# Where four stationary operands lie in SBUF: a two-layer decoder trunk with the start addresses of xh, xl, yh and yl moved by 16 to 64 bytes

## The chip, the cores and the metric

The kernel runs on one core of a Trainium2 chip. The metric is the device time in microseconds of one execution. Before the change the median of three runs is 935.96 us (935.75 to 936.89).

## The reference

The reference computes a causal decoder trunk of two layers over 256 positions of width 2,048, in float32. Cut to what matters:

```python
def layer_even(x, norm_g, w_in, w_out):          # layer 0
    h = rmsnorm(x, norm_g)
    qa, ka, va, iq, ik, iw, qb, kb, vb, gate = split_cols(h @ w_in, SPLIT0)
    ...                                          # mixer A: top-64 sparse attention, 10 heads
    ...                                          # mixer B: dilated windows, 6 heads
    y = jnp.concatenate([o_a, o_b], axis=-1)
    return x + (y * jax.nn.silu(gate)) @ w_out

def layer_odd(x, norm_g, w_in, b_f, w_out):      # layer 1
    ...                                          # the same with stick-breaking and forgetting attention
    return x + (y * jax.nn.silu(gate)) @ w_out

def reference(x, ...):
    x = layer_even(x, norm0, w_in0, w_out0)
    x = layer_odd(x, norm1, w_in1, b_f1, w_out1)
    return rmsnorm(x, norm_f)
```

Nearly all arithmetic is in the four products `h @ w_in` and `y @ w_out`: 256 rows by 2,048 by some 20,000 columns of weights in all.

## The kernel before

**Jobs.** The columns of the four weight matrices are sorted into 39 jobs of mostly 512 columns: 14 for layer 0's input projection (one for each head or pair of heads, K with 336 columns for the shared keys, I0 and I1 for the indexer), P0 to P3 for its output projection, 17 for layer 1's input projection (F1 with 264 columns and G1 with 256 among them), and Q0 to Q3 for its output projection. `project` (L303) runs a job: 16 k tiles of 128, for each of them two tiles of 128 positions (`th`).

**The product.** A float32 product is made of three single-pass products in the type fp32r. A weight tile is split into a high and a low part, `whi` and `wlo`, by ScalarE (L265) and VectorE (L266), two k tiles at a time; the input has been split in the same way into `xh` and `xl` (inputs of both input projections) or `yh` and `yl` (inputs of both output projections). `product` (L298 to L301) then issues

```python
nc.tensor.matmul(o, a, wh, ...)   # L299: a = xh or yh
nc.tensor.matmul(o, a, wl, ...)   # L300: a = xh or yh
nc.tensor.matmul(o, b, wh, ...)   # L301: b = xl or yl
```

The second argument, 128 x 128 of the input, is the stationary operand: it is loaded into the array ahead of each matmul (LDWEIGHTS rows, PEld in the profile). The third, a row of split weights (a "row" is one k tile of a job: 512 columns, 2,048 bytes in a partition), is streamed through. There is such a load for each matmul, since two neighbours never share one instruction. The loads of x and y tiles take 128 x 4 = 512 bytes out of each partition, those of neighbouring `th` and k lying 512 bytes apart.

**Where it lies.** The Tile pools hand out SBUF in the order of the code. Before, `align_bytes=PHASE` with PHASE = 512 puts the four inputs at multiples of 512 bytes in a partition, and a tile `fill` of 88 floats (L209) brings the weights' buffers `raw`, `whi` and `wlo` behind them to multiples of 512 as well. The rows in `whi` and `wlo` follow one another without a gap, so every row of 512 or 256 columns starts at a multiple of 512; every second row of F1 (264 columns, 1,056 bytes) starts 32 over one, every second row of K (336 columns, 1,344 bytes) 320 over. The indexer's `ih` and `il` (loaded at L530 to L532) lie 192 over. In bytes from the start of a partition, with the rest against 512:

| tile | before | rest | after | rest |
|---|---|---|---|---|
| xh | 16,896 | 0 | 16,864 | 480 |
| xl | 33,792 | 0 | 33,312 | 32 |
| yh | 50,688 | 0 | 50,112 | 448 |
| yl | 67,584 | 0 | 66,576 | 16 |
| cons, xs | 83,968, 96,256 | 0 | 82,976, 95,264 | 32 |
| raw, first whi, first wlo | 115,200, 139,776, 156,160 | 0 | 114,688, 139,264, 155,648 | 0 |

**Order of the work.** The order is written by hand (`manual_schedule`). While `project` walks through a job, `tick` advances the attention work of earlier jobs, which is written as generators and yields its instructions between the job's matmuls: transposes (L357, L603), scores, weighted sums. Splits run three halves ahead (AHEAD, L295). The room of yh and yl serves in the first job as landing place for eight k tiles of weights each (`home`, tiles w0yh and w0yl), and yh and yl are allocated over it once that job is done (L773). In the last job, Q3, the room of xh and xl takes split weights of the first eight k tiles (L256 to L258), and the second tile of positions is done in two halves of 256 columns.

Of the kernel before, what the change touches and what calls it, by code (L numbers as in the profile page):

```python
# [7 lines left out]
F32 = mybir.dt.float32  # L8
BF16 = mybir.dt.bfloat16
F32R = mybir.dt.float32r  # L10
# [4 lines left out]
P = 128  # L15
NT = 2
SEQ = 256
D = 2048
KT = D // P
# [133 lines left out]
    t = np.concatenate([t, ci, si], 1)  # L153
    return np.ascontiguousarray(t.reshape(NT, P, -1).transpose(1, 0, 2).reshape(P, -1))

PHASE = 512


@with_exitstack
def trunk(ctx, tc, x, xT, g1, w0, wo0, w1, wo1, bf, gf, consts, rope, out):  # L160
    nc = tc.nc
    cp = ctx.enter_context(tc.tile_pool(name="cp", bufs=1))
# [4 lines left out]
    pa = ctx.enter_context(tc.tile_pool(name="pa", bufs=2, space=PSUM))  # L167
    ctx.enter_context(tc.manual_schedule())

    xh, xl = (cp.tile([P, KT, SEQ], F32R, name=n, align_bytes=PHASE) for n in ("xh", "xl"))  # L170
    home = [cp.tile([P, KT * SEQ], F32, name=f"w0{n}", tag=n, align_bytes=PHASE) for n in ("yh", "yl")]
    ys = []
    cons = cp.tile([P, CW], F32, name="cons")
    rt = cp.tile([P, NT, RW // 2], F32, name="rt")
# [31 lines left out]
    logf = cp.tile([P, NT, HDD], F32, name="logf")  # L206
    cq = cp.tile([P, NT, HDD], F32, name="cq")
    cT = score[0:HDD, 0:SEQ]
    cp.tile([P, 88], F32, name="fill")  # L209
    cTd = dr.tile([HDD, SEQ], F32, name="cTd")  # L210
    r0, r1, r2 = rstd[:, 0, :], rstd[:, 1, :], rstd[:, 2, :]
    BLK = ((0, slice(0, P)), (1, slice(P, 384)))
# [62 lines left out]
    def start(g):  # L275
        n = next(g, None)
        if n is not None:
            side.append([g, n])
# [24 lines left out]
    def project(ji):  # L303
        _, (w, _), name, which = jobs[ji]
        ah, al = ys if which else (xh, xl)
        ps = [pj.tile([P, 512], F32, name=f"pj{th}", tag=f"pj{th}") for th in range(NT)]
        mine = [i for i in range(hidx[0], len(halves)) if halves[i][0] == ji]
        hidx[0] = mine[-1] + 1

        def kts(i, ths, cs=slice(0, w)):  # L310
            _, _, kt0, _, m = halves[i]
            hi, lo = parts[i]
            for j in range(m):
                kt = kt0 + j
                for th in ths:
                    t = slice(th * P, (th + 1) * P)
                    product(ps[th][:, cs], ah[:, kt, t], al[:, kt, t], hi[:, j * w:(j + 1) * w][:, cs],
                            lo[:, j * w:(j + 1) * w][:, cs], kt)
                tick(w * len(ths) / 2)

        if name == "Q3":
            for i in mine:
                split(i + 1 + AHEAD)
                kts(i, (0,))
            finish(ps, 0)
            for c2 in range(2):
                if c2:
                    ps[1] = pj.tile([P, 512], F32, name="pj1", tag="pj1")
                for i in mine:
                    kts(i, (1,), slice(c2 * 256, (c2 + 1) * 256))  # L330
                tail(ps, c2)
            finish(ps, 1)
            return ps
        for i in mine:
            split(i + 1 + AHEAD)
            kts(i, (0, 1))
        return ps
# [126 lines left out]
    def norm0():  # L464
        for th in range(NT):
            for c in range(4):
                sumsq(0, th, c)
                if c % 2:
                    yield 1
        norm(0)  # L470
        for th in range(NT):
            nc.vector.tensor_scalar(rt[:, th, :], rt[:, th, :], r0[:, th:th + 1], None, op0=OP.mult)
        nc.vector.tensor_scalar(hr0, r0, 0.5, None, op0=OP.mult)

    def head_b(ps, h):
        qk = hp.tile([P, 512], F32, name="qk", tag="qk")
        v = hp.tile([P, NT, P], F32, name="v", tag="v")
        u = hp.tile([P, SEQ], F32, name="u", tag="u")
        tg = hp.tile([P, SEQ], F32, name="tg", tag="tg")
        for th in range(NT):  # L480
            t = slice(th * P, (th + 1) * P)
            rotate(qk[:, th * 256:(th + 1) * 256], ps[th][:, 0:256], rt[:, th, 0:256], rt[:, th, 256:512], 1, 256)
            nc.scalar.activation(tg[:, t], ps[th][:, 384:512], AF.Tanh, scale=hr0[:, th:th + 1])
            nc.scalar.activation(v[:, th], ps[th][:, 256:384], AF.Copy, scale=r0[:, th:th + 1])
        for th in range(NT):
            t = slice(th * P, (th + 1) * P)
            nc.vector.scalar_tensor_tensor(u[:, t], tg[:, t], 1.0, ps[th][:, 384:512], op0=OP.add, op1=OP.mult)
        yield 4
        t = qk_turned([qk[:, 0:P], qk[:, P:256], qk[:, 384:512], qk[:, 256:384]])
        yield 2  # L490
        yield from softmax_head(qk_of(t), bmask, [v[:, 0], v[:, 1]], u, hr0, YPOS[f"B{h}"])

    def keys_a(ps):
        kr = hp.tile([P, 512], F32, name="kr", tag="qk")
        for th in range(NT):
            rotate(kr[:, th * P:(th + 1) * P], ps[th][:, 0:P], rt[:, th, P:2 * P], rt[:, th, 3 * P:4 * P], 1, P)
            o = 256 + th * P
            rotate(kr[:, o:o + DI], ps[th][:, 256:320], rt[:, th, 512:576], rt[:, th, 576:640], 1, DI)
            nc.gpsimd.tensor_copy(kr[:, o + DI:o + P], kr[:, o:o + DI])
            nc.scalar.activation(vA[:, th, :], ps[th][:, P:2 * P], AF.Copy, scale=r0[:, th:th + 1])  # L500
            nc.vector.tensor_scalar(iw[:, th, :], ps[th][:, 320:336], r0[:, th:th + 1], None, op0=OP.mult)
        yield 4
        pt = turn([kr[:, i * P:(i + 1) * P] for i in range(4)])
        nc.scalar.activation(kA, pt[:, 0:P], AF.Copy)
        nc.scalar.activation(kAh, pt[:, 0:256], AF.Copy)
        nc.vector.tensor_tensor(kAl, pt[:, 0:256], kAh.bitcast(F32), op=OP.subtract)
        for j in range(2):
            d = slice(j * DI, (j + 1) * DI)
            nc.scalar.activation(ikh[d, j], pt[d, 256:512], AF.Copy)
            nc.vector.tensor_tensor(ikl[d, j], pt[d, 256:512], ikh[d, j].bitcast(F32), op=OP.subtract)  # L510
# [43 lines left out]
    def both(a, b):  # L554
        yield from a
        yield from b
# [60 lines left out]
    def scaled_qk(ps, sgn):  # L617
        qk = hp.tile([P, 512], F32, name="qk", tag="qk")
        for th in range(NT):
            nc.scalar.activation(qk[:, th * 256:th * 256 + P], ps[th][:, 0:P], AF.Copy, scale=rr[:, sgn, th:th + 1])  # L620
            nc.vector.tensor_scalar(qk[:, th * 256 + P:(th + 1) * 256], ps[th][:, P:256], r1[:, th:th + 1], None,
                                    op0=OP.mult)
        return qk
# [145 lines left out]
    for ji, (_, _, name, _) in enumerate(jobs):  # L769
        ps = project(ji)  # L770
        k, h = name[0], int(name[1:] or 0)
        if name == "B0":
            ys += [cp.tile([P, KT, SEQ], F32R, name=n, tag=n, align_bytes=PHASE) for n in ("yh", "yl")]  # L773
            nc.gpsimd.memset(ikh.bitcast(F32), 0.0)
            nc.gpsimd.memset(ikl.bitcast(F32), 0.0)
        if name == "I1":
            nc.gpsimd.dma_start(gn1, g1)
            nc.gpsimd.dma_start(bfs, bf)
        if name == "P0":
            sph = hp.tile([P, 512], F32R, name="sph", tag="ih", bufs=1)  # L780
            spl = hp.tile([P, 512], F32R, name="spl", tag="il", bufs=1)
            for t in (sph, spl):
                nc.gpsimd.memset(t[:, 0:P].bitcast(F32), 0.0)
            tt = hp.tile([P, 2, P], F32R, name="tris", tag="vt", bufs=1)
            nc.scalar.preload_act_table_set("natural_log_exp_and_others")
            tris = [tt[:, 0], tt[:, 1]]
            nc.scalar.activation(tris[0], ntri, AF.Copy)
            nc.scalar.activation(tris[1], nones, AF.Copy)
        if name == "D1":
            for c in range(2):  # L790
                gb.append(hp.tile([P, 1024], F32, name="gb", tag=("ih", "il")[c], bufs=1))
                nc.gpsimd.dma_start(gb[c], gf[:, c * 1024:(c + 1) * 1024])
        if name == "B0":
            start(both(norm0(), head_b(ps, 0)))
        elif k == "B":
            start(head_b(ps, h))
        elif k == "K":
            start(keys_a(ps))
        elif k == "I":
            start(both(index(ps, h), best()) if h else index(ps, h))  # L800
        elif k == "A":
            start(heads_a(ps, h))
        elif k == "P":
            start(feed1(ps, h))
        elif k == "F":
            held = scaled_qk(ps, 0)
            start(forget(ps))
        elif k == "G":
            start(head_cf(ps, held))
        elif k == "C":  # L810
            start(head_c(ps, h))
        elif k == "D":
            start(head_d(ps, h))
        elif k == "Q" and h < 3:
            residual(ps, 2, h)
        if name == "C7" or (k == "D" and h < HDD - 1):
            start(delay(forget_bias(h + 1 if k == "D" else 0), 1))
# [33 lines left out]
```

## Time and profile before

| | |
|---|---|
| median of 3 runs | 935.96 us |
| the profiled execution | 937.04 us |
| its span, first to last instruction | 935.3 us |
| its granted TensorE clock, mean | 0.996 |
| TensorE busy, matmuls / weight loads | 923.2 / 774.6 us |
| VectorE / ScalarE / GpSimd busy | 591.0 / 479.1 / 43.8 us |
| L299 with xh, x992 | 389.5 us busy, 393 ns each |
| L300 with xh, x992 | 379.4 us busy, 382 ns each |
| L301 with xl, x992 | 380.1 us busy, 383 ns each |
| L299, L300, L301 with yh, yl, x248 each | 96.1, 94.9, 95.0 us busy |
| moved by DMA | 168.76 MB, 180 GB/s on average |

The profiled execution is 1.08 us longer than the median of the runs, and 1.7 us of it lie outside the span. Matmuls are pipelined: one begins before the last has ended, so the lengths in the table add up to more than the span. How fast TensorE really goes is the way from one start to the next in the timeline. With the last job's rows that stream out of xh and xl (x24 on each line) the trace has 3 x (992 + 248 + 24) = 3,792 matmuls of L299 to L301.

### The profile page before, as it was taken

What the parts mean: (1) busy time and instruction counts of PE and PEld (TensorE: products, weight loads), DVE (VectorE), ACT (ScalarE), POOL (GpSimd) and SP (SyncE); (2) the same over time, 40 slices, a digit from 0 to 9 for tenths busy, and PEclk for the clock granted to TensorE, in tenths of its full rate; (3) what the DMA queues carried; (4) which work ended last, traced back from release to release, by engine and by line L of the source; (5) the groups of instructions that cost most, each with busy time, mean ns of one, the idle gap of its engine ahead of it and who ended that gap; (6) DMA issues with size and microseconds to landing.
All of it is one profiled execution on the core that took longest, in us unless ns stands there. A gap on an engine that the chain in (4) does not pass through costs nothing.

```text
span 935.3 us, 11922 instructions
## 1 busy us (share of the span) xinstructions
PE 923.2 (99%) x4538; PEld 774.6 (83%) x4538; DVE 591.0 (63%) x978; ACT 479.1 (51%) x804; POOL 43.8 (5%) x63
## 2 busy tenths in 40 slices
PE   9999999999999999999999999999999999999996
PEld 6888888888888888888898888888888888888886
DVE  7467777766565665555567666666766666665553
ACT  7554454445445555545455555555555545554451
POOL 0002100000000000000000000000000000001110
PEclk9999999999999999999999999999999999999999
DMA  9765354444455445555346444445655555455542
GB/s 350 286 224 181 135 176 171 168 168 139 170 180 180 141 175 180 180 180 180 131 167 242 162 159 163 168 175 180 231 186 184 171 172 176 176 180 180 181 179 90
DMA packets 27177, 168.76 MB, mean 180 GB/s; under 512 B 3160, under 2 KB 3696, under 8 KB 8944
## 3 DMA queue, kind: packets, MB, share of 16 engines
q1 hardware_dynamic: 25920, 165.10, 50.1%
q0 software_dynamic: 768, 2.12, 0.8%
q8 instruction: 35, 0.57, 0.2%
q10 hardware_dynamic: 432, 0.79, 0.2%
q14 instruction: 22, 0.18, 0.1%
HBM read 165.89 MB, written 2.11 MB: 180 GB/s over the span
## 4 chain that ended last, share of the span: by engine, by line
PE 91%; DMA 2%; DVE 2%; issue 2%; ACT 2%; SPq 0%; POOL 0%; POOLq 0%; ACTq 0%; DVEq 0%
PE pj L301 27%; PE pj L299 27%; PE pj L300 27%; PE tp L357 3%; DMA raw<-in_w_in_dram 1%; DMA w0yh<-in_w_in_dram 1%; PE o L385 1%; PE o L384 1%; PE o L383 1%; ACT sq L423 1%; PE s L400 1%; DVE wlo L266 0%; PE s L373 0%; PE s L372 0%; PE s L374 0%
## 5 line engine op out<-in xcount | busy, mean ns | idle before, releaser
L266 DVE TENSOR_TENSOR wlo<-raw,whi 128x1024 fp32r<-128x1024 f32 (+3 forms) x300 | 356.2, 1198 | 221.0 <-ACT whi L265 220.8
L265 ACT ACTIVATE whi<-raw 128x1024 fp32r<-128x1024 f32 (+3 forms) x300 | 304.8, 1026 | 170.3 <-PE pj L301 154.9
L299 PE MATMUL pj<-whi,xh 128*128 128x512 f32 (+3 forms) x992 | 389.5, 393 | 0.5 <-ACT whi L265 0.5
L301 PE MATMUL pj<-whi,xl 128*128 128x512 f32 (+3 forms) x992 | 380.1, 383 | 0.0
L300 PE MATMUL pj<-wlo,xh 128*128 128x512 f32 (+3 forms) x992 | 379.4, 382 | 0.1
L301 PEld LDWEIGHTS pj<-whi,xl 128*128 128x128 f32 x992 | 187.4, 189 | 36.6
L299 PEld LDWEIGHTS pj<-whi,xh 128*128 128x128 f32 x992 | 187.8, 189 | 32.1 <-ACT whi L265 1.5
L300 PEld LDWEIGHTS pj<-wlo,xh 128*128 128x128 f32 x992 | 188.0, 189 | 31.4 <-DVE wlo L266 0.9
L299 PE MATMUL pj<-whi,yh 128*128 128x512 f32 (+1 forms) x248 | 96.1, 388 | 0.0
L301 PE MATMUL pj<-whi,yl 128*128 128x512 f32 (+1 forms) x248 | 95.0, 383 | 0.0
L300 PE MATMUL pj<-wlo,yh 128*128 128x512 f32 (+1 forms) x248 | 94.9, 383 | 0.0
L301 PEld LDWEIGHTS pj<-whi,yl 128*128 128x128 f32 x248 | 46.6, 188 | 9.2
L299 PEld LDWEIGHTS pj<-whi,yh 128*128 128x128 f32 x248 | 46.7, 188 | 8.6
L300 PEld LDWEIGHTS pj<-wlo,yh 128*128 128x128 f32 x248 | 46.7, 188 | 8.6
L409 ACT ACTIVATE pr<-sn,nm 128x128 f32<-128x128 f32 (+1 forms) x48 | 21.5, 448 | 46.4 <-DVE nm L407 46.4
L393 ACT ACTIVATE yh<-tp 128x256 fp32r<-128x256 f32 x32 | 12.3, 384 | 46.6 <-PE tp L357 46.6
L634 DVE RECIPROCAL e<-e 128x256 f32<-128x256 f32 x16 | 28.1, 1753 | 0.5
L352 POOL TENSOR_TENSOR qk<-rot,rot 128x256 f32<-128x256 f32 x22 | 16.0, 737 | 238.2 <-DVE rot L351 238.2
L423 ACT ACTIVATE sq<-xs 128x512 f32<-128x512 f32 x23 | 14.3, 623 | 22.7 <-DVE xs L591 22.5
L394 DVE TENSOR_TENSOR yl<-tp,yh 128x256 fp32r<-128x256 f32 x32 | 13.5, 423 | 19.5 <-ACT yh L393 19.3
L366 ACT ACTIVATE qkh<-tp 128x384 fp32r<-128x384 f32 x22 | 10.8, 491 | 20.1 <-PE tp L357 20.0
L620 ACT ACTIVATE qk<-pj,rr 128x128 f32<-128x128 f32 x32 | 11.7, 367 | 15.7 <-PE pj L301 15.7
(201 smaller groups left out, 704.1 us busy)
## 6 DMA issues: line engine op xcount, KB each, us to landing
raw<-in_w_in_dram SPq DMA_DIRECT2D x108, 1024.0 KB, 4.8
raw<-in_w_out_dram SPq DMA_DIRECT2D x32, 1024.0 KB, 4.8
raw<-in_w_in_dram SPq DMA_DIRECT2D x4, 672.0 KB, 11.5
raw<-in_w_in_dram SPq DMA_DIRECT2D x4, 528.0 KB, 3.5
w0yl<-in_w_in_dram SPq DMA_DIRECT2D x4, 512.0 KB, 7.0
xs<-in_x_dram SPq DMA_DIRECT2D x2, 1024.0 KB, 11.8
raw<-in_w_in_dram SPq DMA_DIRECT2D x4, 512.0 KB, 3.9
xst<-in_xT_dram SPq DMA_DIRECT2D x6, 256.0 KB, 6.3
```

The source lines that it names most:

```text
L265: nc.scalar.activation(hi, rw, AF.Copy)
L266: nc.vector.tensor_tensor(lo, rw, hi.bitcast(F32), op=OP.subtract)
L299: nc.tensor.matmul(o, a, wh, start=(kt == 0), stop=False)
L300: nc.tensor.matmul(o, a, wl, start=False, stop=False)
L301: nc.tensor.matmul(o, b, wh, start=False, stop=(kt == KT - 1))
L352: nc.gpsimd.tensor_tensor(dst, t1[:, 0:n], t2[:, 0:n], op=OP.add)
L357: nc.tensor.transpose(pt[:, i * P:(i + 1) * P], s, ident)
L393: nc.scalar.activation(yh[:, kt, :], pt[:, 0:SEQ], AF.Copy)
L394: nc.vector.tensor_tensor(yl[:, kt, :], pt[:, 0:SEQ], yh[:, kt, :].bitcast(F32), op=OP.subtract)
L409: nc.scalar.activation(pr[:, s], sn[:, s], AF.Exp, scale=-1.0, bias=nm[:, th:th + 1], accum_out=l[:, th:th + 1])
L423: nc.scalar.activation(j, xs[:, th, c * 512:(c + 1) * 512], AF.Square, accum_out=ss[:, i, th, c:c + 1])
L634: nc.vector.reciprocal(e, e)
```

## The change

The four inputs get start addresses of their own, given as rests against 512 in a table PHASES: 480 for xh, 32 for xl, 448 for yh, 16 for yl. Since the pool hands out room in steps of 32 bytes, a filler tile ahead of each input brings its base to a multiple of 32, and yl is made 4 floats longer and used from its fifth float on. The filler ahead of the weights' buffers grows from 88 to 208 floats, which keeps them at multiples of 512. No instruction is added, taken away or moved, and the order on all five engines is the same; what changes is the addresses in the table above, and with them the lines of the code behind the change by 9 to 11.

```diff
-PHASE = 512
+PHASES = {"xh": 480, "xl": 32, "yh": 448, "yl": 16}
...
-    xh, xl = (cp.tile([P, KT, SEQ], F32R, name=n, align_bytes=PHASE) for n in ("xh", "xl"))
-    home = [cp.tile([P, KT * SEQ], F32, name=f"w0{n}", tag=n, align_bytes=PHASE) for n in ("yh", "yl")]
+    at, first = 128, {}
+    for n, ph in PHASES.items():
+        base = ph // 32 * 32
+        if base != at:
+            cp.tile([P, (base - at) % 512 // 4], F32, name=f"fill_{n}")
+        x_in = n[0] == "x"
+        first[n] = cp.tile([P, KT * SEQ + ph % 32 // 4], F32R if x_in else F32, name=n if x_in else f"w0{n}", tag=n)
+        at = (base + ph % 32 + 31) // 32 * 32 % 512
+    xh, xl = (first[n].rearrange("p (a b) -> p a b", a=KT) for n in ("xh", "xl"))
+    home = [first[n][:, PHASES[n] % 32 // 4:] for n in ("yh", "yl")]
...
-    cp.tile([P, 88], F32, name="fill")
+    cp.tile([P, 208], F32, name="fill")
...
-            ys += [cp.tile([P, KT, SEQ], F32R, name=n, tag=n, align_bytes=PHASE) for n in ("yh", "yl")]
+            for n in ("yh", "yl"):
+                pad = PHASES[n] % 32 // 4
+                ys.append(cp.tile([P, KT * SEQ + pad], F32R, name=n, tag=n)[:, pad:].rearrange("p (a b) -> p a b", a=KT))
```

## The prediction

> **What bounds the kernel now.** I read the page's busy times and its chain first, then TensorE's waits.
>
> ```profile
> PE 923.2 (99%) x4538; PEld 774.6 (83%) x4538; DVE 591.0 (63%) x978; ACT 479.1 (51%) x804; POOL 43.8 (5%) x63
> PE 91%; DMA 2%; DVE 2%; issue 2%; ACT 2%; SPq 0%; POOL 0%; POOLq 0%; ACTq 0%; DVEq 0%
> PE tp L357 <- POOL qk L352: 2.0, 2, 1.8
> PE s L761 <- DVE mhalf L762: 1.2, 1, 1.2
> PE pj L299 <- ACT whi L265: 0.5, 1, 0.5
> PE pj L300 <- DVE xl L266: 0.3, 1, 0.3
> ACT whi L265 <- PE pj L301: 154.9, 107, 2.6
> ```
>
> The end is set by TensorE's own stream: its four waits come to 4.0 us. The engines that split the weights wait for it, not the other way round (last row). So the change can act on the time only through the pace of the matmuls. That pace is read from starts, not from the busy column, since matmuls overlap. The timeline of TensorE in the output projection P (start in us, length in us), where nothing interrupts it, with two weight loads from the weight-load rows below it:
>
> ```profile
> 424.16 0.39 PE L299 MATMUL pj<-whi,yh 128*128 128x512 f32 x1
> 424.39 0.39 PE L300 MATMUL pj<-wlo,yh 128*128 128x512 f32 x1
> ...
> 425.52 0.39 PE L299 MATMUL pj<-whi,yh 128*128 128x512 f32 x1
> 424.17 0.19 PEld L300 LDWEIGHTS pj<-wlo,yh 128*128 128x128 f32 x1
> 424.39 0.19 PEld L301 LDWEIGHTS pj<-whi,yl 128*128 128x128 f32 x1
> ```
>
> Six starts in 1.36 us: 226.7 ns for 512 columns. The weight load for the next matmul begins as the current one begins, so TensorE reads SBUF twice at once: 2,048 bytes of split weights per partition, and 512 bytes of xh, xl, yh or yl. Two other stretches tell how much of the 226.7 ns is streaming: the last job's 256-column half (12 rows, first and last) and the first job's opening (6 rows).
>
> ```profile
> 915.65 0.28 PE L299 MATMUL pj<-xh,yh 128*128 128x256 f32 x1
> ...
> 916.97 0.28 PE L301 MATMUL pj<-xh,yl 128*128 128x256 f32 x1
> 7.12 0.63 PE L299 MATMUL pj<-whi,xh 128*128 128x512 f32 x1
> ...
> 9.25 0.63 PE L301 MATMUL pj<-whi,xl 128*128 128x512 f32 x1
> ```
>
> The halves start every 1.32 / 11 = 120.0 ns. So 256 columns cost 106.7 ns, a column 0.417 ns, 512 columns 213.4 ns, and each matmul carries 13.3 ns more, whatever its width. In the opening the array still runs at half pace, and there a matmul takes 2.13 / 5 = 426 ns, twice 213: no extra at all. An extra that is gone when columns are read at half speed looks like two reads in each other's way, not like a fixed price of changing weights. The Trainium skill, "TensorE: Matmul & The Clock Gate", section "Back-to-back issue gap", gives N / 2.4 + 2.5 ns, which would be 215.8 ns here; the trace has 226.7 ns, so the measurement decides, and by the page's figure there would be an estimated 10.9 ns per matmul that its formula does not hold.
>
> **The change part by part.** Instructions, their order and their waits are the same on all five engines; only addresses differ. The program has 3,792 of these matmuls: 38 jobs of 16 x 2 x 3 = 96, and 48 + 96 in the last, whose second half is cut in two. One ns on each is 3.79 us, 0.4% of the profiled 937.04 us. All 13.3 ns together are 50 us, the most that any address could win.
>
> *The common shift of everything behind the inputs.* The weights' buffers move 512 bytes down and stay at multiples of 512. cons, rt, xs and the small tiles stand 32 bytes further on against 512; no row of before shows a price for that, and ACT and DVE have 49% and 37% of the span idle. Nothing.
>
> *yl at 16 bytes over, as a landing place.* Four pieces of the first job land there.
>
> ```profile
> 15.40 1.22 DVE L266 TENSOR_TENSOR wlo<-w0yl,whi 128x1024 fp32r<-128x1024 f32 x1
> 18.92 0.39 PE L299 MATMUL pj<-whi,xh 128*128 128x512 f32 x1
> DMA to landing us min/median/max: 6.9/7.0/7.2
> ```
>
> The first split of such a piece ends at 16.62, and the first matmul that uses it (the 49th of the job) starts at 18.92. So a landing of 7.0 us may become 2.3 us longer before TensorE waits. Nothing, and beyond that cover one for one.
>
> *The relative address of the two reads.* This is the change. Before, every load of xh, xl, yh, yl and nearly every row of split weights begins at a multiple of 512. After, loads begin at -32 (xh), +32 (xl), -64 (yh), +16 (yl), while the streamed rows stay where they were, except in the last job, which streams out of xh and xl. What another relative address costs cannot be read off the main stream, which knows one. But some places of before already differ. (a) F1 has rows of 264 columns, 1,056 bytes: every second one is streamed from 32 over a multiple of 512, so the loads lie 32 under it. (b) K has 336 columns, 1,344 bytes: every second row is 320 over. (c) In the indexer the loads come from 192 over. (d) Behind other work the addresses are equal, but the timing is disturbed. First and last rows of (a), 40 rows; of (b), 13; three rows of (c); of (d) the first matmul behind other work, the next five, and what follows them:
>
> ```profile
> 475.22 0.28 PE L301 MATMUL pj<-whi,xl 128*128 128x264 f32 x1
> ...
> 479.97 0.29 PE L301 MATMUL pj<-whi,xl 128*128 128x264 f32 x1
> 35.80 0.32 PE L299 MATMUL pj<-whi,xh 128*128 128x336 f32 x1
> ...
> 37.65 0.32 PE L299 MATMUL pj<-whi,xh 128*128 128x336 f32 x1
> 85.42 0.39 PE L530 MATMUL s<-ikh,ih 128*128 128x512 f32 x1
> 85.65 0.39 PE L531 MATMUL s<-ikl,ih 128*128 128x512 f32 x1
> 85.88 0.39 PE L532 MATMUL s<-ikh,il 128*128 128x512 f32 x1
> 426.56 0.48 PE L299 MATMUL pj<-whi,yh 128*128 128x512 f32 x1
> 426.88 0.40 PE L300 MATMUL pj<-wlo,yh 128*128 128x512 f32 x1
> ...
> 427.80 0.39 PE L301 MATMUL pj<-whi,yl 128*128 128x512 f32 x1
> 428.04 0.60 PE L603 MATMUL tp<-cons,xs 128*128 128x128 f32 x4
> ```
>
> (a) 4.75 / 39 = 121.8 ns, less 264 x 0.417 = 110.0: an extra of 11.8 ns, 1.5 under the main stream. (b) 1.85 / 12 = 154.2 less 140.0: 14.2 ns, 0.9 over. (c) 0.46 / 2 = 230 ns: 3.3 over. (d) 1.16 / 5 = 232 ns: 5.3 over. So the extra is no constant: with address and timing it moves by some ns both ways, and the main stream's even 226.7 is a state into which equal addresses settle. The shortest that single matmuls reach is in their lengths (the lines view of short windows: 477.80 to 477.89, then 427.60 to 427.79; the steady length is the median row):
>
> ```profile
> L301 PE MATMUL pj<-whi,xl 128*128 128x264 f32 x1 | 0.3, 278 | 0.0
> L300 PE MATMUL pj<-wlo,yh 128*128 128x512 f32 x1 | 0.4, 387 | 0.0
> L301 PE MATMUL pj<-whi,xl x992: 274/389/628, 6.7 to 836.3; 128*128 128x512 f32 x180, 128*128 128x264 f32 x7, 128*128 128x336 f32 x6, 128*128 128x256 f32 x6
> ```
>
> A record is 389 - 227 = 162 ns longer than the way to the next start. So 278 is a step of 116 ns with 264 columns, an extra of 6 ns, 7.3 under the main stream; 387 is 2.0 under it. Both ends: -7.3 ns on all, -27.7 us; +5.3 ns (d), +20.1 us.
>
> I take -2.0 ns. The row nearest to the change is (a): its 32 bytes under are xh's offset, and xl's with the other sign; these two are loaded in 31 of 39 jobs. It has that offset in half of its rows only and is still 1.5 ns better; 2.0 is what a 512-column matmul has shown itself to reach. The sum: 3,792 x 2.0 = 7.6 us, 937.04 - 7.6 = 929.4 us profiled. The profiled execution stands 1.08 us over the median of the runs, so 928.3, forecast 928.
>
> What is next late: splitting follows TensorE (154.9 us of waiting for it), so 8 us less leaves it in time. The first matmul behind a change of kind (0.32 us from 426.56 to 426.88) has other causes and stays.
>
> **The rivals.**
>
> *Slower: the stream never settles.* With equal addresses every load meets the stream in the same way, and the steps come to rest at 226.7 ns. With four offsets the meeting place jumps by 64 or 80 bytes between a high and a low load, and the stream may run for good in what it passes through now in (c) and (d). For it: (b) and (c), with unequal addresses, are dearer. Against it: (a). Prices: (b) 0.9 x 3.79 = 3.4 us, 939.4 on the median's footing; (c) 3.3 x 3.79 = 12.5 us, 948.5. It decides as soon as the mean step is over 226.7 ns. Chance 0.29; of these I hold two thirds for under 945.
>
> *No change: the extra is fixed.* The 13.3 ns are a price of swapping weights, and (a) to (d) only show disturbed timing. Then the steps stay 226.7, and the time 936.0. For it: 512 and 256 columns have the same extra to 0.1 ns. Against: it is missing at half pace, and (a) and (b) differ without a disturbance. Chance 0.13. The same page of the Trainium skill, in "Step-by-step: what each phase is for", would have it so: "Loading the next tile's weights doesn't steal SBUF read bandwidth from the running matmul." By that rule addresses cannot matter, and this rival would be certain; the rows (a) and (b) speak against it.
>
> *Much faster: the offsets keep the reads apart.* If loads and stream stay out of each other's way as in the 116 ns step throughout, 27.7 us go, 908. For it is one row; a mean seldom equals a minimum. Chance 0.08 for under 912, which is an extra of 7 ns, 6.3 x 3.79 = 23.9 us less, inside the faster case.
>
> **How the numbers follow.** Faster, with steps under 226.7: 0.58, likeliest at 928, from 912 to 934 by itself. No change 0.13, slower 0.29. About 0.2%, or 1.9 us, is what a measurement of this kernel can tell. The range reaches from 912 to 945: below it 0.08, above it a third of the slower case, 0.10.
>
> **What would show it.** The step between starts in an uninterrupted stretch of P and of a layer's middle: under 226.7 ns, about 224.7, if I am right; 226.7 in the same even pattern if the extra is fixed; 228 to 232, uneven, if the stream no longer settles. The median length of L299 to L301 rows tells the same: 387 against 389. xh, xl and yh, yl may part, since their offsets differ: then the median of the yh rows goes another way than that of the xh rows. The prediction is wrong if TensorE's waits grow beyond 4 us, or if the steps stay and the time does not.

## The result: 1.05% slower

The changed kernel takes 946.0 us (median of 4 runs, 945.38 to 946.7) against 936.1 us before: a ratio of 1.0105, 95% interval 1.0087 to 1.0122. The forecast was 928 us, range 912 to 945. Its profiled execution has 945.38 us and a span of 943.6 us at a mean granted clock of 0.997.

TensorE still sets the end, and still hardly waits. Its waits after (us in total, times, longest):

```profile
PE pj L308 <- ACT whi L274: 1.6, 2, 0.9
PE s L770 <- DVE mhalf L771: 1.2, 1, 1.2
PE pj L309 <- DVE wlo L275: 1.0, 2, 0.8
PE s L382 <- DVE qkl L377: 0.5, 1, 0.5
```

4.3 us in all, where it was 4.0. So the time is in the pace. The timeline of TensorE after, in an uninterrupted stretch of the output projection (loads of yh and yl), then one of layer 1 (loads of xh and xl), then the 256-column half of the last job:

```profile
421.62 0.40 PE L308 MATMUL pj<-whi,yh 128*128 128x512 f32 x1
421.86 0.39 PE L309 MATMUL pj<-wlo,yh 128*128 128x512 f32 x1
422.09 0.39 PE L310 MATMUL pj<-whi,yl 128*128 128x512 f32 x1
...
423.69 0.40 PE L308 MATMUL pj<-whi,yh 128*128 128x512 f32 x1
594.02 0.39 PE L310 MATMUL pj<-whi,xl 128*128 128x512 f32 x1
...
596.80 0.40 PE L310 MATMUL pj<-whi,xl 128*128 128x512 f32 x1
923.88 0.28 PE L308 MATMUL pj<-xh,yh 128*128 128x256 f32 x1
...
925.18 0.28 PE L310 MATMUL pj<-xh,yl 128*128 128x256 f32 x1
```

Nine steps in 2.07 us are 230 ns, twelve in 2.78 us are 232 ns; both were 226.7. The steps repeat here too: in the second stretch they run twice, to within 1 ns, through 231, 236, 231, 231, 229 and 229 ns. Eleven steps in 1.30 us are 118 ns for 256 columns, where they were 120. The median lengths say the same: 389 ns before, and after (tile xl, tile yl; shortest, median, longest):

```profile
L310 PE MATMUL pj<-whi,xl x992: 277/393/628, 6.5 to 843.8; 128*128 128x512 f32 x180, 128*128 128x264 f32 x7, 128*128 128x336 f32 x6, 128*128 128x256 f32 x6
L310 PE MATMUL pj<-whi,yl x248: 278/391/400, 356.7 to 935.1; 128*128 128x512 f32 x116, 128*128 128x256 f32 x8
```

From the starts of all matmuls of L299 to L301 (L308 to L310 after), the mean step by the kind of load and by the place behind the last other work on TensorE; steps with a wait in them are left out:

| steps | count | before, ns | after, ns | difference, us |
|---|---|---|---|---|
| 512 columns, xh or xl, from the tenth on | 1,334 | 227.3 | 231.4 | +5.5 |
| the same, second to ninth | 1,175 | 229.4 | 231.7 | +2.7 |
| the same, first | 157 | 287.7 | 288.7 | +0.2 |
| 512 columns, yh or yl, from the tenth on | 583 | 226.9 | 229.8 | +1.7 |
| the same, second to ninth | 119 | 229.6 | 230.4 | +0.1 |
| 256 columns, from the tenth on | 155 | 119.9 | 117.8 | -0.3 |

The sum is 9.9 us, as the medians' 9.9. Of the uninterrupted steps with xh or xl from the tenth on, 1,138 of 1,218 belonged to the even 226, 227, 227 ns before, and none does after; with yh or yl it is 556 of 572 and 3. The two profiled spans differ by 8.3 us only, since their openings differ: the indexer's first job begins at 49.6 us before and at 48.6 us after. From there to the end it is 885.7 and 895.0 us, 9.3 us more.

The opening after also has a stretch in which the profile records a granted clock of 0.50 (the column behind GpSimd's `0.00 (x0)`):

```profile
12.50:15.30 2.80, 2.80 (x8) 2.21 (x7) 2.80 (x5) 2.59 (x5) 0.00 (x0) 0.50 1.03 413
12.82 0.63 PE L308 MATMUL pj<-whi,xh 128*128 128x512 f32 x1
...
14.95 0.62 PE L310 MATMUL pj<-whi,xl 128*128 128x512 f32 x1
```

Five steps in 2.13 us are 426 ns, as in the opening of before, although the loads here are off level: in this stretch at half clock the step has neither the 13.3 ns nor the price of the offset.

### The profile page after: what moved, and what is told of

Its sections match the earlier page's. It is cut to its first block, busy times and chain, and to the rows that moved or that the text cites. A ratio compares the mean times of both kernels' runs of the same rounds, so it can differ in the third digit from the quotient of the medians.

```text
span 943.6 us, 11922 instructions
## 1 busy us (share of the span) xinstructions
PE 930.9 (99%) x4538; PEld 772.4 (82%) x4538; DVE 591.7 (63%) x978; ACT 479.9 (51%) x804; POOL 43.9 (5%) x63
## 4 chain that ended last, share of the span: by engine, by line
PE 94%; DVE 2%; issue 1%; ACT 1%; DMA 1%; SPq 0%; POOLq 0%; POOL 0%; ACTq 0%; DVEq 0%
PE pj L308 29%; PE pj L309 28%; PE pj L310 28%; PE tp L366 3%; PE o L393 1%; PE o L394 1%; PE o L392 1%; DMA w0yh<-in_w_in_dram 1%; DVE wlo L275 1%; PE s L409 1%; PE s L382 0%; PE s L381 0%; PE s L383 0%; PE tp L612 0%; PE s L541 0%
## 5 line engine op out<-in xcount | busy, mean ns | idle before, releaser
L308 PE MATMUL pj<-whi,xh 128*128 128x512 f32 (+3 forms) x992 | 391.5, 395 | 1.6 <-ACT whi L274 1.6
L309 PE MATMUL pj<-wlo,xh 128*128 128x512 f32 (+3 forms) x992 | 381.1, 384 | 1.0 <-DVE wlo L275 1.0
L310 PE MATMUL pj<-whi,xl 128*128 128x512 f32 (+3 forms) x992 | 381.1, 384 | 0.0
L310 PEld LDWEIGHTS pj<-whi,xl 128*128 128x128 f32 x992 | 186.7, 188 | 40.0
L308 PEld LDWEIGHTS pj<-whi,xh 128*128 128x128 f32 x992 | 186.9, 188 | 35.7 <-ACT whi L274 2.9
L309 PEld LDWEIGHTS pj<-wlo,xh 128*128 128x128 f32 x992 | 187.1, 189 | 34.4 <-DVE wlo L275 1.9
L308 PE MATMUL pj<-whi,yh 128*128 128x512 f32 (+1 forms) x248 | 97.1, 392 | 0.0
L309 PE MATMUL pj<-wlo,yh 128*128 128x512 f32 (+1 forms) x248 | 95.3, 384 | 0.0
L310 PE MATMUL pj<-whi,yl 128*128 128x512 f32 (+1 forms) x248 | 95.2, 384 | 0.0
L310 PEld LDWEIGHTS pj<-whi,yl 128*128 128x128 f32 x248 | 46.6, 188 | 10.3
L308 PEld LDWEIGHTS pj<-whi,yh 128*128 128x128 f32 x248 | 46.6, 188 | 8.9
L309 PEld LDWEIGHTS pj<-wlo,yh 128*128 128x128 f32 x248 | 46.6, 188 | 8.7
L403 DVE TENSOR_TENSOR yl<-tp,yh 128x256 fp32r<-128x256 f32 x32 | 13.5, 422 | 20.1 <-ACT yh L402 20.1
```

The source lines that it names most:

```text
L308: nc.tensor.matmul(o, a, wh, start=(kt == 0), stop=False)
L309: nc.tensor.matmul(o, a, wl, start=False, stop=False)
L310: nc.tensor.matmul(o, b, wh, start=False, stop=(kt == KT - 1))
L403: nc.vector.tensor_tensor(yl[:, kt, :], pt[:, 0:SEQ], yh[:, kt, :].bitcast(F32), op=OP.subtract)
```

## The experiments

The working theory after the result is the prediction's slower rival, in two forms. U: the offsets are unequal, and the stream never settles because high and low load lie differently against it. O: any load that is not level with the streamed row keeps it from settling, equal or not. Rivals: C, the shift of all the other tiles; and from the prediction, a fixed price of changing weights. Jobs that load xh and xl and jobs that load yh and yl do not touch each other's steps, so each run tests two settings. "Level" means that a load starts at the same rest as the row that is streamed. Where nothing else is said, the filler ahead of the weights' buffers (`fill`) is set anew in each run so that the streamed rows stay at multiples of 512.

**All four off level, in equal pairs.**

```diff
-PHASES = {"xh": 480, "xl": 32, "yh": 448, "yl": 16}
+PHASES = {"xh": 32, "xl": 32, "yh": 64, "yl": 64}
```

> xh and xl both at 32 over a multiple of 512, yh and yl both at 64 over; streamed rows stay at 0. Theory U (unequal loads: the steps settle when every load lies alike against the stream, and do not when high and low load lie differently): steps come to rest at 226.7 ns as before, time 936 us. Theory O (offset: any load that is not level with the streamed row costs, equal or not): steps of 229 to 232 ns in the 512-column jobs, time 943 to 947 us.

951.92 us, ratio 1.0171 (1.0154 to 1.0188). The output projection there (uninterrupted, timeline of TensorE):

```profile
421.33 0.39 PE L310 MATMUL pj<-whi,yl 128*128 128x512 f32 x1
421.56 0.40 PE L308 MATMUL pj<-whi,yh 128*128 128x512 f32 x1
421.80 0.39 PE L309 MATMUL pj<-wlo,yh 128*128 128x512 f32 x1
422.03 0.40 PE L310 MATMUL pj<-whi,yl 128*128 128x512 f32 x1
422.26 0.39 PE L308 MATMUL pj<-whi,yh 128*128 128x512 f32 x1
422.49 0.40 PE L309 MATMUL pj<-wlo,yh 128*128 128x512 f32 x1
...
423.43 0.40 PE L310 MATMUL pj<-whi,yl 128*128 128x512 f32 x1
```

Steps of 236 and 231 ns take turns, nine in 2.10 us: 233.3 on average, and 233.2 in the jobs with xh and xl. It does come to a steady pattern, but to a dearer one. Theory U is out: equal offsets are worse than the change's unequal ones. O holds, and its price was set a little low (943 to 947 us, 229 to 232 ns).

**The change for xh and xl alone.**

```diff
+PHASES = {"xh": 480, "xl": 32, "yh": 0, "yl": 0}
```

> The change made for xh and xl alone (480 and 32); yh and yl stay at 0. If the relative address of load and stream is the cause (U or O), the jobs that load xh and xl step at 231.4 ns as in the changed kernel, the jobs that load yh and yl at 226.7 to 226.9, and the time is about 2 us under the changed kernel's, 943.5 to 944.5 us. A third theory, C (the common shift of all other buffers costs), has every job slow or none: 946 us, or 936.

943.32 us, ratio 1.0081 (1.0066 to 1.0096). Jobs with xh and xl step at 231.4 ns as in the changed kernel, the uninterrupted output projection at 226.7. So 7.5 of the 9.9 us come from xh and xl, and some 2.4 to 2.7 from yh and yl. C would have had all jobs slow or none.

**The low parts alone.**

```diff
+PHASES = {"xh": 0, "xl": 32, "yh": 0, "yl": 16}
```

> Only the low parts move: xl to 32 over, yl to 16 over; xh and yh stay at 0. Theory U: the steps no longer settle, 229 to 232 ns in both kinds of jobs, 942 to 947 us. Theory O: only the matmul under which xl or yl is loaded (L309) is longer, by 3 to 13 ns, the other two stay at 226.7; 938 to 952 us, told apart by which line carries it.

950.39 us, ratio 1.0155 (1.014 to 1.0171), over U's 942 to 947: one load of three off level is about as bad as three. By line, with xl at 32: L308 232.3, L309 238.7, L310 228.4 ns. L309, under which xl is loaded, carries most, as O says, but its neighbours, under which xh is loaded from 0, do not stay at 226.7 either. So a disturbed step tells on its neighbours; how is not shown. With yl at 16 the three lines have 230.7, 233.4 and 232.2 ns.

**Loads half as long.** All inputs at 0; in 14 of 16 k tiles the loads take 64 of 128 columns, which leaves out the product for half of the positions there.

```diff
 def product(o, a, b, wh, wl, kt):
+        if 0 < kt < KT - 1:
+            o, a, b = o[0:64], a[:, 0:64], b[:, 0:64]
```

> All four at 0 as before, but in 14 of the 16 k tiles only 64 of the 128 columns of xh, xl, yh, yl are loaded, which leaves out the product for half of the positions there; the streamed rows are unchanged. If the 13.3 ns are loads and stream in each other's way, a load half as long costs about half: steps of about 220 ns, time 913 to 918 us. If they are a fixed price of changing weights, steps stay 226.7 ns and the time 936 us.

939.85 us, ratio 1.0043 (1.0028 to 1.0059): slower, which neither had. Weight loads are 134 ns long instead of 188, yet the steps have a mean of 229.6 ns. An uninterrupted stretch of P1 (25 rows, first and last):

```profile
388.04 0.40 PE L311 MATMUL pj<-wlo,yh 128*64 128x512 f32 x1
...
393.56 0.40 PE L311 MATMUL pj<-wlo,yh 128*64 128x512 f32 x1
```

24 steps in 5.52 us are 230.0 ns; they run through 236, 229, 224, 227, 234 and 230 over and over. So the 13.3 ns are not in proportion to what is loaded, and the half loads of this stretch come to rest in another pattern than 226, 227, 227. The shorter load is not the only difference: such a matmul also writes 64 partitions instead of 128.

**Scans of the rest.** All inputs at 0; each of 26 jobs takes its loads of xh and xl from another place further on.

```diff
-                    product(ps[th][:, cs], ah[:, kt, t], al[:, kt, t], ...
+                    product(ps[th][:, cs], off(ah, kt, th, 0), off(al, kt, th, 1), ...
+        def off(a, kt, th, part):
+            s = kt * SEQ + th * P + (0 if which else REST.get(name, (0, 0))[part] // 4)
+            return a.rearrange("p a b -> p (a b)")[:, min(s, KT * SEQ - P):][:, 0:P]
```

> All four inputs at 0, but 26 jobs of 512 columns that load xh and xl take their loads from 0, 4, 8, 16, 24, 32, 48, 64, 80, 96, 112, 128, 144, 160, 192, 224, 256, 288, 320, 352, 384, 416, 448, 464, 480 and 496 bytes further on (one value for each job, the same for xh and xl, in the order of the jobs), which multiplies by other positions and dims of the input than the reference does; instructions, order and waits are those of before. Theory O1 (level is the only rest that settles): 226.7 ns in the job with 0, 229 to 235 in all others. Theory O2 (the rest counts against a shorter period, 128 or 256 bytes): 226.7 also at the multiples of that period, and the values repeat with it. Theory O3 (0 is a good rest but not the best): some rests step below 226, by 2 ns or more.

> The same with the load of xl alone moved by those 26 values, xh at 0 (again other positions and dims than the reference's for xl). O1: 226.7 in the job with 0 alone; the line under which xl is loaded carries most of the rest, 238 to 239 ns at 32. O2: repeats with 128 or 256. O3: some rests under 226.

> The same with the load of xh alone moved by those 26 values, xl at 0 (other positions and dims than the reference's for xh). Two of three loads are now off level. O1: 226.7 in the job with 0 alone, 229 to 236 in the others. O2: repeats with 128 or 256. O3: some rests under 226.

Mean step in ns, from the ninth matmul behind other work on; the equal scan also has the rest 256 further on. Each scan is one execution, and each value the mean of one job's 27 to 58 steps:

| rest, bytes | both moved | both, 256 more | xl alone | xh alone |
|---|---|---|---|---|
| 0 | 227.0 | 227.1 | 226.9 | 227.0 |
| 4 | 232.4 | - | 232.6 | 230.9 |
| 16 | 228.7 | - | 231.6 | 228.0 |
| 32 | 233.1 | 233.4 | 233.1 | 232.0 |
| 64 | 233.2 | 233.2 | 231.2 | 231.3 |
| 96 | 233.7 | 233.8 | 233.6 | 230.3 |
| 128 | 232.8 | 231.8 | 230.9 | 232.7 |
| 160 | 233.3 | 233.3 | 233.3 | 231.1 |
| 192 | 229.7 | 229.3 | 231.2 | 229.5 |
| 256 | 227.1 | - | 226.7 | 226.9 |
| 496 | 228.3 | - | 227.3 | 231.2 |

Two uninterrupted stretches of the equal scan, job C6 with a rest of 256 (24 rows, first and last) and C7 with 288 (23 rows, the last of them already other work):

```profile
605.81 0.39 PE L309 MATMUL pj<-whi,xh 128*128 128x512 f32 x1
...
611.02 0.39 PE L311 MATMUL pj<-whi,xl 128*128 128x512 f32 x1
630.81 0.40 PE L311 MATMUL pj<-whi,xl 128*128 128x512 f32 x1
...
635.94 0.34 PE L707 MATMUL s<-sph,tris 128*128 128x384 f32 x1
```

5.21 / 23 = 226.5 ns and 5.13 / 22 = 233.2 ns. The values come back after 256 bytes, to about 1 ns: O2 holds, with that period. None lies under 226; O3 is out. In the equal scan 55 of 58 steps at 0 and 45 of 51 at 256 belong to the even 226, 227, 227 ns, and none at 4, 32, 64, 96, 128, 160 or 192. Some rests do both: 35 of 51 steps at 16 are even and the others run at 231 to 236 ns, and with xl alone at 496 it is 45 of 51. So the table's values between 227 and 229 are in part mixtures of patterns and not one step.

**Loads and streamed rows moved together.** Weights' buffers at 32, xh and xl at 32, yh and yl at 0.

```diff
+PHASES = {"xh": 32, "xl": 32, "yh": 0, "yl": 0}
-    cp.tile([P, 208], F32, name="fill")
+    cp.tile([P, 96], F32, name="fill")
```

> The weights' buffers and with them all streamed rows go to 32 over a multiple of 512, xh and xl to 32 over as well, yh and yl stay at 0. Theory R (what counts is the load's rest against the streamed row's, counted in 256 bytes): jobs that load xh and xl settle at 226.7 ns, jobs that load yh and yl do not, 228 to 234 ns; time 938 to 941 us. Theory A (what counts is each address against 256 bytes by itself): the jobs with xh and xl do not settle, 229 to 235 ns, time 950 us or more.

939.39 us, ratio 1.0035 (1.0021 to 1.0048). First job of layer 1, loads of xh and xl, from where it has settled (72 rows, first and last), and the job before it, loads of yh and yl:

```profile
453.80 0.39 PE L308 MATMUL pj<-whi,xh 128*128 128x512 f32 x1
...
469.90 0.39 PE L310 MATMUL pj<-whi,xl 128*128 128x512 f32 x1
424.61 0.39 PE L310 MATMUL pj<-whi,yl 128*128 128x512 f32 x1
...
426.71 0.39 PE L310 MATMUL pj<-whi,yl 128*128 128x512 f32 x1
```

71 steps in 16.10 us are 226.8 ns; the jobs of layer 1 with xh and xl have means of 226.6 to 227.3. Nine steps in 2.10 us, 233.3 ns, for yh and yl, which lie at a multiple of 512. So it is the difference between load and streamed row that counts (R), not the address (A); this was tried with a shift of 32 bytes alone. These jobs of y alone cost 3.3 us.

**Pairs, and rests close to level.** The scans' edit, with pairs.

> All four inputs at 0, 26 jobs with loads moved as in the scans before (other positions and dims than the reference's), by pairs for xh and xl: 508/508, 504/504, 500/500, 492/492, 484/484, 252/252, 260/260, 240/240, 272/272, 8/504, 504/8, 496/16, 16/496, 480/32, 448/16, 32/480, 16/448, 0/508, 508/0, 0/504, 504/0, 256/256, 0/256, 256/128, 128/384, 240/256. If level against 256 bytes is the whole story: 226.7 for 256/256 and 0/256 alone, 227 to 234 for all others, 480/32 at the 231.4 and 448/16 at the 229.8 ns of the changed kernel although cons, xs and all other tiles lie as before. If a rest just under a multiple of 256 is better than level: 508, 504 or 252 under 226.

256/256 has 226.6 and 0/256 226.9 ns. 480/32 has 231.2, and 448/16 229.8, the changed kernel's own 231.4 and 229.8, although all other tiles lie as before: the addresses of the loads are the whole change. An uninterrupted stretch of the job with 480/32 (22 rows, first and last), 4.86 / 21 = 231.4 ns:

```profile
532.67 0.39 PE L311 MATMUL pj<-whi,xl 128*128 128x512 f32 x1
...
537.53 0.39 PE L311 MATMUL pj<-whi,xl 128*128 128x512 f32 x1
```

Just under level is no better: 508 has 233.2, 504 232.9, 500 233.0, 492 231.7, 252 233.2. The best off level in this scan are 496/16 with 227.6 and 0/508 with 227.7, again mixtures (34 of 43 and 27 of 51 steps are even); the worst is 504/0 with 234.3.

**Loads of any length.** By job, 128 down to 8 columns; for the other positions the product is left out in 14 of 16 k tiles.

```diff
+        if n < P and 0 < kt < KT - 1:
+            o, a, b = o[0:n], a[:, 0:n], b[:, 0:n]
```

> All four inputs at 0; in 14 of 16 k tiles the loads take only 128, 120, 112, 104, 96, 88, 80, 72, 64, 56, 48, 40, 32, 24, 16, 8 and again 128, 112, 96, 80, 64, 48, 32, 16, 64, 32 columns of the input, by job, which leaves out the product for the other positions there. If the 13.3 ns grow with the length of the load, steps fall from 226.7 towards 213 to 216 ns as the load gets shorter. If they are a price of changing weights and the timing of starts only, steps stay between 224 and 236 ns, and settle at 226.7 in some jobs and not in others.

128 columns have 226.8 and 227.1 ns in two jobs; 112 have 228.6 and 230.0, 96 have 230.0 and 229.9, 64 have 229.7, 229.3 and 228.8, 48 have 233.5 and 234.1, 32 have 231.6, 231.5 and 231.0, 16 have 231.3 and 229.8, 8 have 229.4. A weight load of 8 columns and the matmuls around it, then a later stretch of the same job (19 rows, first and last):

```profile
576.70 0.09 PEld L312 LDWEIGHTS pj<-wlo,xh 128*8 128x8 f32 x1
576.69 0.39 PE L311 MATMUL pj<-whi,xh 128*8 128x512 f32 x1
...
578.51 0.39 PE L313 MATMUL pj<-whi,xl 128*8 128x512 f32 x1
581.38 0.40 PE L311 MATMUL pj<-whi,xh 128*8 128x512 f32 x1
...
585.54 0.40 PE L311 MATMUL pj<-whi,xh 128*8 128x512 f32 x1
```

The load is 0.09 us instead of 0.19. Eight steps take 1.82 us, 228 ns to the rounding of the rows; one by one they are 226 and 227 ns, the even step of full loads. In the later stretch 18 steps take 4.16 us, 231.1 ns: loads of the same length at the same rests, in another pattern. So the settled step does not depend on the length of the load (8 columns or 128), nothing falls towards 213, and what shorter loads change is how often the stream comes to the even pattern: 19 of 51 steps with 8 columns, none with 72, against 56 of 58 and 45 of 51 with 128. The second expectation holds but for its upper bound: with 48 columns single steps reach 240 ns.

**Level against 256 instead of 512.** xh and yl at 256, nothing left out.

```diff
+PHASES = {"xh": 256, "xl": 0, "yh": 0, "yl": 256}
```

> xh and yl at 256 over a multiple of 512, xl and yh at 0; nothing left out. If level means a multiple of 256 and the shift of the other tiles costs nothing: steps of 226.7 ns in all jobs and a time within 0.2% of before, 934.5 to 937.5 us. If only multiples of 512 are level: as the changed kernel, 943 to 947 us.

936.21 us, ratio 1.000 (0.9991 to 1.0009): the time of before, with another layout. No version beats the kernel before; among the rests tried, level has the shortest mean step.

## Why the prediction was wrong

- **The place** was right: TensorE's waits stayed at some 4 us, and nearly the whole difference is in the step of the 512-column matmuls. That addresses matter was right too; the rival of no change is out. Its rule in the Trainium skill ("TensorE: Matmul & The Clock Gate", section "Step-by-step: what each phase is for") says that a weight load takes no SBUF read bandwidth from the running matmul. The runs agree in so far as the length of the load does not matter: in its even stretch the job with loads of 8 columns steps at 226 and 227 ns, as with 128. But they contradict the use I put it to: the place that a load comes from does change the step, by up to 7 ns.
- **The step that failed** is "I take -2.0 ns. The row nearest to the change is (a)". Row (a), F1, has 264 columns, and what 264 columns do says nothing of 512. Its steps hardly depend on the setting: 121.0 ns before, 121.4 with the change, 120.9 with xh and xl both at 32, from the tenth step on. So the -2.0 ns of the sum stand against +4.1 ns (xh, xl) and +2.9 ns (yh, yl) from the tenth step on. After the change its 38 steps below take 4.61 us, 121.3 ns, as against 121.8 in the row quoted before:

```profile
478.97 0.28 PE L308 MATMUL pj<-whi,xh 128*128 128x264 f32 x1
...
483.58 0.28 PE L310 MATMUL pj<-whi,xl 128*128 128x264 f32 x1
```

  At 256 columns off level is even 2 ns shorter (119.9 to 117.8), at 512 it is 4 ns longer. I compared by offset and should have compared by form: the only rows of 512 columns off level were (c), 3.3 ns over, and they had the sign. Their steps of 229, 232 and 226 ns are those that the equal scan runs through at the same rest of 192. Row (b) was no sample either: K's rows of 336 columns have 154.2 ns before and after. With (a) and (b) the prediction also spoke against the rival of no change, and these two rows do not move with the loads' start (F1 has 120.5 to 122.2 ns over all runs, K 153.8 to 154.4 wherever whole loads are used), so that part of the argument was right by luck. Why narrow rows behave otherwise is not shown.
- **The 387 ns record** as what a 512-column matmul "has shown itself to reach" was no bound for a mean. Short steps stand among long ones: 224 right behind 236 in the settling rows of before, and 224 with 236 in the half-load pattern.
- **The rival that happened** was priced at 939.4 and 948.5 us and measured 946.0: the mechanism it names, a stream that does not come to rest at 226.7, is what the steps show, though they repeat a dearer pattern and its reason was wrong. It is not that the loads differ from each other (equal ones at 32 are worse, 0 and 256 are as good as equal), but that any is off level. Its prices, 0.9 and 3.3 ns, stand against the same 4.1 and 2.9 ns; of the two, the one from (c) was near.
- **The reading of 13.3 ns** as two reads in each other's way is not borne out: it does not shrink with the load. What it is stays open, and so is why the relative address counts in 256 bytes. That 512 and 256 columns have the same extra was no finding of its own, since the column's price came from the same two steps; half of the opening's 426 ns, 213, gives 13.7 and 13.5 ns and bears it out. That it is missing at half pace still stands: the granted clock does not show it for the opening of before (1.00 from 7.0 to 9.5 us, though a step takes 426 ns), but the stretch at 0.50 after does.
- **The costs put at nothing** were so: the other tiles' shift (480/32 and 448/16 have the changed kernel's steps with cons, xs and the small tiles as before, and the 256 layout has them 256 further on and the same time), and the landing of four pieces at yl, 7.1 us instead of 7.0.

## What to carry to other kernels

Where a matmul of 512 fp32r columns is streamed over and over with a new stationary operand each time, look at the steps between starts, not at busy times: an even step is a settled state, and the layout can lose it. Here loads that start level with the streamed row, to a multiple of 256 bytes, settle at 226.7 ns, and others end in patterns, or in mixtures of patterns, of 227 to 234 ns on average; the dearest layout cost 1.7% of the whole kernel. And a row of another width is no stand-in for the one that is priced, however alike its offset: take the rows of the same form first.

## What the runs showed that was not expected

- The step depends on the rest of the load's start against the streamed row's start, with a period of 256 bytes; rests of 16, 32 or 64 bytes, natural choices for staggering, cost 1 to 6 ns at full clock, and nothing in the one stretch at a granted clock of 0.50.
- One off-level load in three lengthens all three steps (232.3, 238.7, 228.4 ns).
- At 256 columns the same offsets shorten the step by 2 ns.
- The step is not fixed by the setting alone: with loads of 8 columns one job runs at 226 and 227 ns in one stretch and at 231.1 in a later one, at the same rests. Half loads, 64 of 128 columns, have a mean of 229.6 ns even when level.
